# A decoder layer in fp32: how the down projection's weight sums are stored and split, and from which queue gate/up's results are stored

## The chip, the cores and the metric

The kernel runs on one core of a Trainium2 chip. The metric is the device time of one execution in microseconds (us). A core has five engines that work side by side, each through its own list of instructions in order: TensorE (PE) multiplies, VectorE (DVE) and ScalarE (ACT) do element-wise work, GpSimd (POOL) does some of it too, and SyncE (SP) mostly issues transfers. Transfers can be issued from SP, ACT and POOL. An engine that meets an instruction whose inputs are not ready waits there, with everything behind it.

## The reference

One layer of a hybrid decoder runs over 512 prompt tokens and 8 decode tokens, all in float32, with a model width of 2048 and an FFN width of 5632:

```
h = h + [gated delta net(x) ; multi-scale pooling(x)] @ w_out      with x = rmsnorm(h)
h = h + (silu(x2 @ w_gate) * (x2 @ w_up)) @ w_down                 with x2 = rmsnorm(h)
y = rmsnorm(h)
```

The outputs are y for both sets of tokens and the new recurrent, convolution and pooling states. The change touches the second line alone: gate/up is a product of 520 tokens with 2048 x 11264 weights, down one with 5632 x 2048.

## The kernel before, in words

Every float32 operand is split in two parts, hi (a copy rounded to the PE's format, cast by ACT, L1263) and lo (what is left, a subtraction by DVE, L1264). A product is then three passes: hi by hi, hi by lo, lo by hi (`passes`, L1270 to L1272), each a matmul of a 128 x 128 weight block with 260 tokens. Both FFN products use Strassen's scheme in Winograd's form: a pair of output columns times two halves of the tokens is computed with seven products M1 to M7 instead of eight. The weight sides of these are A11, A12, A22 and the sums S1 to S4 (made by DVE in `add`, L1299); the activation sides are B11, B21, B22 and T1 to T4, called forms (`FORM`). `strassen` (L1409) runs the products; at product i it cuts (splits into hi and lo) the weight of product i + 3 and makes the sum for i + 4, and at products 0, 2, 3 and 4 of a pair SP issues the loads A21, A11, A22 and A12 of the next pair. A pair is seven products, of 24 matmuls each in gate/up.

Gate/up has 22 blocks of FFN columns, each with a gate pair and an up pair (`gu`). After the up pair DVE multiplies the two (`gated`, L1460), POOL makes the four T forms of the result by subtraction (`to_dram`, L1466 to L1468) and stores all eight forms in DRAM (`a_d`, L1469, 1040 KB), issued from POOL. `hidden` is the hook that places this and other side work between products.

The down projection is cut along its inner dimension into three parts of 7, 7 and 8 blocks (`SIZES`), each with eight pairs. The forms of a part are loaded from `a_d` by `fetch` (L1824) and split by `fill` (ACT L1833, DVE or POOL L1835). So that forms can be replaced, the last pair of a stage is computed as eight plain products (`plain`), and meanwhile `cross` fetches and splits the next forms. There are three such crossings: from gate/up to part 0, and between the parts. The first pair of a part uses sums made ahead: during gate/up `sums_ahead` loads its blocks, makes S1 to S4 and stores seven blocks in DRAM (`near_d`); at the crossing SP reads them back (L1288), and they are split there and during that first pair, which goes in the order M4, M7, M1, M6, M5, M2, M3. In the first crossing the last `gated` and `to_dram` run too, and behind them POOL issues the loads of the residual h_d (`residual`, L2120: 12 of 260 KB, eight into mixb, four into mixa, which still holds what L1469 stores).

Names in the profile: raw, hi and lo are weight blocks (three buffers each, plus a fourth set from `xcp`); sg also holds A21; mixa and mixb are large buffers used for several things; dn and mm are PE's output banks; b11, b21, B22 and T1 to T4 with h or l are the forms.

Of the kernel before, what the change touches and what calls it, by code (L numbers as in the profile page):

```python
# [8 lines left out]
F32 = mybir.dt.float32  # L9
# [60 lines left out]
def decoder_kernel(ctx, tc, x_prompt, x_sample, state_delta, state_conv, state_pool, norm_mix, w_in,  # L70
# [1173 lines left out]
    BLOCKS = ("A11", "A12", "A22", "S1", "S2", "S3", "S4")  # L1244
# [4 lines left out]
    near_d = dram.tile([len(SIZES), 7, P, HG * P], F32, name="near_d")  # L1249
# [24 lines left out]
    class Pair:  # L1274
# [6 lines left out]
        def load(self, name, t=None):  # L1281
            if self.near is None:
                self.raw[name] = load_raw(self.view(int(name[1]) - 1, int(name[2]) - 1), t)
                return
            if t is None:
                t = wpl.tile([P, HG * P], F32, tag="raw", name="raw")
            self.raw[name] = t[:, :self.width]
            sp.dma_start(self.raw[name], self.near[BLOCKS.index(name), :, :self.width])  # L1288

        def cut(self, name, pool_=wpl):  # L1290
            self.w[name] = cut_raw(self.raw[name], pool_)

# [116 lines left out]
    def strassen(pairs, r21, hook, extra, order=FIRST):  # L1409

        steps = [(q, n) for q in range(len(pairs)) for n in (
            CROSSED if pairs[q].near is not None else order if q == len(pairs) - 1 else STEADY)]

        def block(i):
            return (pairs[steps[i][0]], FORM[steps[i][1]][0]) if i < len(steps) else (None, "")

        for i, (q, n) in enumerate(steps):  # L1420
            j = i % 7
            hook(q, j)
            if q + 1 < len(pairs):
                swap = q + 2 == len(pairs) and order is FIRST
                name = {0: "A21", 2: "A11", 3: "A12" if swap else "A22", 4: "A22" if swap else "A12"}.get(j)
                if name:
                    pairs[q + 1].load(name, r21 if name == "A21" else None)
            (p, name), (p4, name4) = block(i + 3), block(i + 4)
            pool_ = extra if i % 4 == 0 else wpl
            if p4 and p4.near is not None:  # L1430
                name4 = ""
            lastly = isinstance(p4 or p, LastPair)
            if name4 in ("S1", "S2", "S3") and not lastly:
                p4.add(name4)
            if name and (name != "S4" or lastly):
                p.cut(name, pool_)
            if name4 == "S4" or name4[:1] == "S" and lastly:
                p4.add(name4)
            pairs[q].multiply(n)
            pairs[q].combine(n)  # L1440
            if name == "S4" and not lastly:
                p.cut(name, pool_)
# [20 lines left out]
    def to_dram(fp):  # L1463
# [5 lines left out]
        pool.dma_start(a_d[:, :, fp, :].rearrange("q p c -> p q c"), q)  # L1469
# [336 lines left out]
    gu[2].add("S3")  # L1806
    up_out(0, 0, cm[:, 0, :], h1[0])
    gu[2].cut("A22")
    gu[2].load("A12")
    up_out(0, 1, cm[:, 0, :], c1[0])  # L1810
    gu[2].cut("S3")
# [15 lines left out]
    def fill(name, part_, rs=range(0, HG, 2), high=True, eng=dve):  # L1827
        hi, lo = forms[name]
        for r in rs:
            x = slice(r, min(r + 2, SIZES[part_]))  # L1830
            raw = lo[:, x, :].bitcast(F32)
            if high:
                act.copy(hi[:, x, :], raw)  # L1833
            if eng:
                eng.tensor_tensor(lo[:, x, :], raw, hi[:, x, :].bitcast(F32), op=ALU.subtract)  # L1835
# [68 lines left out]
    def run(pairs, r21, hook=None, order=FIRST, last=None, part_=None):  # L1904

        def during(q, j):
            if hook:
                hook(q, j)
            if pairs[0].near is not None and q == 0:
                if j == 2:  # L1910
                    fill("B21", part_)
# [10 lines left out]
    def ahead_of_cross(j, part_, last, r21):  # L1922
# [7 lines left out]
        elif j < 5:  # L1930
            fetch({2: "T4", 3: "T3", 4: "T2"}[j], part_) if j > 1 else None
        elif j == 5:
            first.load("A22")
            last.cut("A11")
            fill("T4", part_)
# [6 lines left out]
    def cross(part_, last):  # L1942
# [3 lines left out]
        def hook(step):  # L1946
# [3 lines left out]
            elif step == 1:  # L1950
                fill("B11", part_, eng=None)
            elif step == 2:
                first.cut("A22")
                fetch("T1", part_)
                fill("B11", part_, (0, 2), False, pool)
            elif step == 3:
                first.cut("S3")
                fetch("B21", part_)
                fill("B11", part_, (4,), False, pool)
            else:  # L1960
                first.cut("A11")
                fetch("B22", part_)
                fill("B11", part_, (6,), False, pool)
# [13 lines left out]
    def sums_ahead(part_):  # L1977
# [6 lines left out]

        def store(name, i):
            sp.dma_start(p.near[BLOCKS.index(name), :, :n], r[i])

        for i, name in enumerate(("A11", "A21", "A22", "A12")):
            sp.dma_start(r[i].rearrange("p (k c) -> p k c", c=P), p.view(int(name[1]) - 1, int(name[2]) - 1))
            yield  # L1990
        yield
        for i, name in ((0, "A11"), (2, "A22"), (3, "A12")):
            store(name, i)
            yield
        for name, *args in (("S3", 1, 0, 1, ALU.subtract), ("S2", 2, 2, 1, ALU.subtract), ("S1", 0, 2, 0, ALU.add),
                            ("S4", 3, 3, 2, ALU.subtract)):
            join(*args)
            yield
            store(name, args[0])

    def hidden(q, j):
# [5 lines left out]
        if j == (1 if q % 2 else 4):  # L2007
# [117 lines left out]
    to_dram(FP - 1)  # L2125
    for part_ in range(1, len(SIZES)):
# [71 lines left out]
```

## Time and profile before

| what | value |
|---|---|
| time, median of 3 runs | 2148.35 us (2147.03 to 2149.63) |
| the profiled execution | 2150.31 us, of which the span (first to last instruction) is 2148.5 us |
| mean granted PE clock | 0.998 |
| PE busy | 2120.6 us, 17680 matmuls |
| DVE, ACT, POOL busy | 1784.7, 934.3, 481.8 us |

W_out, the input projection and the mixing end at about 820 us; gate/up runs from there to about 1655, the first crossing to 1681, then come the parts of the down projection and the crossings between them. In a timeline row the first number is the start, the second the duration, and the bracket at the end holds the time that the engine stood idle before it and what ended that. Where several instructions of one kind follow each other, a row takes them together (x2, x3) and its second number is the time from the first one's start to the last one's end. SPq and POOLq rows are issues of transfers, not the transfers.

### The profile page before, as it was taken

What the parts mean: (1) busy time and instruction counts of PE and PEld (TensorE: products, weight loads), DVE (VectorE), ACT (ScalarE), POOL (GpSimd) and SP (SyncE); (2) the same over time, 40 slices, a digit from 0 to 9 for tenths busy, and PEclk for the clock granted to TensorE, in tenths of its full rate; (3) what the DMA queues carried; (4) which work ended last, traced back from release to release, by engine and by line L of the source; (5) the groups of instructions that cost most, each with busy time, mean ns of one, the idle gap of its engine ahead of it and who ended that gap; (6) DMA issues with size and microseconds to landing.
All of it is one profiled execution on the core that took longest, in us unless ns stands there. A gap on an engine that the chain in (4) does not pass through costs nothing.

```text
span 2148.5 us, 42900 instructions
## 1 busy us (share of the span) xinstructions
PE 2120.6 (99%) x17680; PEld 2106.6 (98%) x17680; DVE 1784.7 (83%) x2647; ACT 934.3 (43%) x1410; POOL 481.8 (22%) x572
## 2 busy tenths in 40 slices
PE   8999999999999999999999999999999999999998
PEld 7999999999999999999999999999999999999998
DVE  7786767666599979989988889888877898988997
ACT  6523443432255444434433434434434445435544
POOL 3212320222012202333233243232121302002100
PEclk9999999999999999999999999999999999999999
DMA  8344434434445535565575556565557737347333
GB/s 283 92 114 113 120 104 113 117 110 109 129 132 161 154 103 142 161 188 158 157 196 166 160 175 186 166 178 149 155 152 230 226 104 241 113 112 273 89 109 119
DMA packets 453569, 325.62 MB, mean 152 GB/s; under 512 B 27836, under 2 KB 424533, under 8 KB 452845
## 3 DMA queue, kind: packets, MB, share of 16 engines
q1 hardware_dynamic: 428781, 240.13, 39.2%
q0 software_dynamic: 23280, 81.94, 12.3%
q8 instruction: 139, 2.28, 0.4%
q10 hardware_dynamic: 1312, 0.80, 0.1%
q14 instruction: 57, 0.47, 0.1%
HBM read 265.76 MB, written 57.72 MB: 151 GB/s over the span
## 4 chain that ended last, share of the span: by engine, by line
PE 80%; DVE 11%; DMA 3%; issue 2%; ACT 2%; POOL 1%; SPq 0%; DVEq 0%; ACTq 0%; POOLq 0%
PE dn L1272 19%; PE dn L1270 19%; PE dn L1271 19%; PE mm L168 6%; PE mm L170 5%; PE mm L169 5%; DVE lo L1264 3%; DVE raw L1299 1%; DMA raw<-in_w_gate_up_dram 1%; DVE lo L137 1%; PE dn L870 1%; ACT hi L1263 1%; DMA qk<-tok_d 1%; DVE xl L195 0%; DMA xt<-in_x_prompt_dram 0%
## 5 line engine op out<-in xcount | busy, mean ns | idle before, releaser
L1264 DVE TENSOR_TENSOR lo<-raw,hi 128x1024 fp32r<-128x1024 f32 (+1 forms) x434 | 558.0, 1306 | 90.2 <-ACT hi L1263 88.7
L1263 ACT CAST hi<-raw 128x1024 fp32r<-128x1024 f32 (+1 forms) x434 | 438.4, 1025 | 427.6 <-DVE raw L1299 239.6
L168 PE MATMUL mm<-xh,hi 128*128 128x256 f32 (+1 forms) x1280 | 377.6, 295 | 2.8 <-DVE mixa L259 2.8
L170 PE MATMUL mm<-xh,lo 128*128 128x256 f32 (+1 forms) x1280 | 362.9, 284 | 0.4 <-DVE lo L137 0.4
L169 PE MATMUL mm<-xl,hi 128*128 128x256 f32 (+1 forms) x1280 | 362.6, 283 | 0.4
L168 PEld LDWEIGHTS mm<-xh,hi 128*128 128x128 f32 x1280 | 242.6, 190 | 6.6 <-DVE mixa L259 3.3
L169 PEld LDWEIGHTS mm<-xl,hi 128*128 128x128 f32 x1280 | 242.8, 190 | 1.0 <-DVE xl L350 1.0
L170 PEld LDWEIGHTS mm<-xh,lo 128*128 128x128 f32 x1280 | 242.0, 189 | 0.6 <-DVE lo L137 0.6
L1299 DVE TENSOR_TENSOR raw<-raw 128x1024 f32<-128x1024 f32 (+1 forms) x130 | 177.2, 1363 | 2.2
L1271 PE MATMUL dn<-b21l,hi 128*128 128x260 f32 x598 | 169.4, 283 | 0.0
L1272 PE MATMUL dn<-b21h,lo 128*128 128x260 f32 x598 | 169.3, 283 | 0.0
L1272 PE MATMUL dn<-b11h,lo 128*128 128x260 f32 x590 | 167.1, 283 | 1.7 <-DVE lo L1264 1.7
L1270 PE MATMUL dn<-b21h,hi 128*128 128x260 f32 x598 | 168.7, 282 | 0.0
L1271 PE MATMUL dn<-b11l,hi 128*128 128x260 f32 x590 | 167.1, 283 | 0.0
L1270 PE MATMUL dn<-b11h,hi 128*128 128x260 f32 x590 | 166.6, 282 | 0.0
L1466 POOL TENSOR_TENSOR mixa<-mixa 128x520 f32<-128x520 f32 x22 | 55.6, 2528 | 461.7 <-DVE mixa L1460 461.7
L1270 PE MATMUL dn<-T1h,hi 128*128 128x260 f32 x534 | 151.9, 284 | 0.0
L1271 PE MATMUL dn<-T1l,hi 128*128 128x260 f32 x534 | 151.5, 284 | 0.0
L1272 PE MATMUL dn<-B22h,lo 128*128 128x260 f32 x526 | 148.6, 283 | 2.6 <-DVE lo L1264 2.6
L1272 PE MATMUL dn<-T1h,lo 128*128 128x260 f32 x534 | 150.6, 282 | 0.0
L135 ACT CAST hi<-raw 128x1024 fp32r<-128x1024 f32 (+2 forms) x86 | 87.2, 1015 | 144.4 <-PE mm L169 141.8
L1270 PE MATMUL dn<-B22h,hi 128*128 128x260 f32 x526 | 149.6, 284 | 0.0
(653 smaller groups left out, 6570.3 us busy)
## 6 DMA issues: line engine op xcount, KB each, us to landing
raw<-in_w_gate_up_dram SPq DMA_DIRECT2D x134, 512.0 KB
raw<-in_w_in_dram SPq DMA_DIRECT2D x79, 512.0 KB
a_d<-mixa POOLq DMA_DIRECT2D x22, 1040.0 KB, 7.7
mixb<-in_w_gate_up_dram SPq DMA_DIRECT2D x41, 512.0 KB
raw<-in_w_down_dram SPq DMA_DIRECT2D x42, 448.0 KB
raw<-in_w_out_dram SPq DMA_DIRECT2D x25, 512.0 KB
raw<-in_w_down_dram SPq DMA_DIRECT2D x21, 512.0 KB
raw<-near_d SPq DMA_DIRECT2D x14, 448.0 KB
```

What stands on the lines that cost most here:

```text
L135: act.copy(hi[:, r], raw[:, r])
L137: dve.tensor_tensor(lo[:, r], raw[:, r], hi[:, r].bitcast(F32), op=ALU.subtract)
L168: te.matmul(acc[ci], wh, hi[k][:, c0:c1], start=(k == 0), stop=False)
L169: te.matmul(acc[ci], wh, lo[k][:, c0:c1], start=False, stop=False)
L170: te.matmul(acc[ci], wl, hi[k][:, c0:c1], start=False, stop=(k == len(w) - 1))
L1263: act.copy(hi, raw)
L1264: dve.tensor_tensor(lo, raw, hi.bitcast(F32), op=ALU.subtract)
L1270: te.matmul(acc, wh[:, k, :], xf[:, k, :], start=start and k == 0, stop=False)
L1271: te.matmul(acc, wh[:, k, :], xg[:, k, :], start=False, stop=False)
L1272: te.matmul(acc, wl[:, k, :], xf[:, k, :], start=False, stop=stop and k == wh.shape[1] - 1)
L1299: dve.tensor_tensor(r[name], r[a], r[b], op=op)
L1466: pool.tensor_tensor(q[:, 4:8:2, :], q[:, 1:4:2, :], q[:, 0:2, :], op=ALU.subtract)
```

## The change

Five things are done. The stored sums: `near_d` holds S1 to S4 only, A11, A12 and A22 of a part's first pair are read from the weights themselves, and `sums_ahead` is spread over other places of gate/up, with its loads and stores behind A12's load. A stored sum is split in place (`cut_sum`): hi goes into a new tile, lo over the raw block. S3 and S2 are split in the crossing, S1, A12 and S4 at the first three products of the first pair. `fill` splits a form in two pieces (blocks 0 to 3, and the rest) instead of four, and all subtractions are DVE's, B11's too, which POOL did before. The store of `a_d` moves from POOL to SP (`keep`): behind the last load (A12) of the next gate pair, and for the last block directly behind `to_dram` in the program. And at the start of gate/up, A22's cut and A12's load come ahead of the addition and the cut of S3.

```diff
-    near_d = dram.tile([len(SIZES), 7, P, HG * P], F32, name="near_d")
+    near_d = dram.tile([len(SIZES), 4, P, HG * P], F32, name="near_d")
...
+        def cut_sum(self, name, pool_=wpl, tag="hi"):
+
+            raw = self.raw[name]
+            hi = pool_.tile([P, HG * P], F32R, tag=tag, name=tag)[:, :raw.shape[1]]
+            act.copy(hi, raw)
+            lo = raw.bitcast(F32R)
+            dve.tensor_tensor(lo, raw, hi.bitcast(F32), op=ALU.subtract)
+            self.w[name] = [x.rearrange("p (k c) -> p k c", c=P) for x in (hi, lo)]
...
+        phase = 0 if pairs[0].near is None else 3
...
-            pool_ = extra if i % 4 == 0 else wpl
+            pool_ = extra if i % 4 == phase else wpl
             if p4 and p4.near is not None:
                 name4 = ""
+            if p and p.near is not None:
+                name = ""
...
-        pool.dma_start(a_d[:, :, fp, :].rearrange("q p c -> p q c"), q)
+
+    def keep(fp):
+        sp.dma_start(a_d[:, :, fp, :].rearrange("q p c -> p q c"), quarters)
...
-    gu[2].add("S3")
-    up_out(0, 0, cm[:, 0, :], h1[0])
     gu[2].cut("A22")
     gu[2].load("A12")
+    gu[2].add("S3")
+    gu[2].cut("S3")
+    up_out(0, 0, cm[:, 0, :], h1[0])
     up_out(0, 1, cm[:, 0, :], c1[0])
-    gu[2].cut("S3")
     gu[2].add("S2")
...
-    def fill(name, part_, rs=range(0, HG, 2), high=True, eng=dve):
+    def fill(name, part_):
         hi, lo = forms[name]
-        for r in rs:
-            x = slice(r, min(r + 2, SIZES[part_]))
+        for x in (slice(0, 4), slice(4, SIZES[part_])):
             raw = lo[:, x, :].bitcast(F32)
-            if high:
-                act.copy(hi[:, x, :], raw)
-            if eng:
-                eng.tensor_tensor(lo[:, x, :], raw, hi[:, x, :].bitcast(F32), op=ALU.subtract)
+            act.copy(hi[:, x, :], raw)
+            dve.tensor_tensor(lo[:, x, :], raw, hi[:, x, :].bitcast(F32), op=ALU.subtract)
...
+                if j == 0:
+                    pairs[0].cut_sum("S1", xcp)
+                if j == 1:
+                    pairs[0].cut("A12")
                 if j == 2:
+                    pairs[0].cut_sum("S4", xcp, "lo")
                     fill("B21", part_)
...
-            elif step == 1:
-                fill("B11", part_, eng=None)
             elif step == 2:
+                fetch("T1", part_)
                 first.cut("A22")
-                fetch("T1", part_)
-                fill("B11", part_, (0, 2), False, pool)
+                fill("B11", part_)
             elif step == 3:
-                first.cut("S3")
                 fetch("B21", part_)
-                fill("B11", part_, (4,), False, pool)
-            else:
+                first.cut_sum("S3")
+                first.cut_sum("S2", tag="lo")
+            elif step == 4:
+                fetch("B22", part_)
                 first.cut("A11")
-                fetch("B22", part_)
-                fill("B11", part_, (6,), False, pool)
                 fill("T1", part_)
...
+        load("A11", 0)
+        load("A21", 1)
+        yield
+        yield
+        yield
+        load("A22", 2)
+        load("A12", 3)
+        yield
+        join(1, 0, 1, ALU.subtract)
+        yield
+        join(2, 2, 1, ALU.subtract)
+        yield
+        store("S3", 1)
+        store("S2", 2)
+        yield
+        join(0, 2, 0, ALU.add)
+        yield
+        join(3, 3, 2, ALU.subtract)
+        yield
+        store("S1", 0)
+        store("S4", 3)
...
+        if j == 5 and q % 2 == 0:
+            keep(q // 2)
+        if j in (1, 2, 5) and q % 2:
...
     to_dram(FP - 1)
+    keep(FP - 1)
```

How the rows move, at three places. First DVE at the start of gate/up, where L1299 (L1305 after) is an addition for a sum, L1264 (L1263) a subtraction for lo and L1450 (L1459) an addition of the up half; before:

```order
L1653 TENSOR_TENSOR T4l<-mixb,T4h 128x520 x2
L1299 TENSOR_TENSOR mixa<-raw,mixa 128x1024
L1450 TENSOR_TENSOR mixa<-cm,dn 128x260
L1264 TENSOR_TENSOR lo<-raw,hi 128x1024
L1450 TENSOR_TENSOR mixa<-cm,mm 128x260
L1264 TENSOR_TENSOR lo<-mixa,hi 128x1024
L1299 TENSOR_TENSOR raw<-raw,mixa 128x1024
L1450 TENSOR_TENSOR mixa<-cm,dn 128x260 x2
L1299 TENSOR_TENSOR raw<-raw 128x1024
L1264 TENSOR_TENSOR lo<-raw,hi 128x1024
L1460 TENSOR_TENSOR mixa<-mixa,sg 128x1040
```

and after:

```order
L1664 TENSOR_TENSOR T4l<-mixb,T4h 128x520 x2
L1263 TENSOR_TENSOR lo<-raw,hi 128x1024
L1305 TENSOR_TENSOR mixa<-raw,mixa 128x1024
L1263 TENSOR_TENSOR lo<-mixa,hi 128x1024
L1459 TENSOR_TENSOR mixa<-cm,dn 128x260
L1459 TENSOR_TENSOR mixa<-cm,mm 128x260
L1305 TENSOR_TENSOR raw<-raw,mixa 128x1024
L1459 TENSOR_TENSOR mixa<-cm,dn 128x260 x2
L1305 TENSOR_TENSOR raw<-raw 128x1024
L1263 TENSOR_TENSOR lo<-raw,hi 128x1024
L1469 TENSOR_TENSOR mixa<-mixa,sg 128x1040
```

The subtraction for A22 has moved to the front, and S3's follows the addition of S3 directly. Next SP over some pairs of gate/up with side work; before:

```order
L1255 DMA raw<-in_w_gate_up_dram 128x8x128 x3
L1255 DMA mixb<-in_w_gate_up_dram 128x8x128
L1255 DMA raw<-in_w_gate_up_dram 128x8x128 x2
L1986 DMA near_d<-mixb 128x896
L1255 DMA raw<-in_w_gate_up_dram 128x8x128
L1255 DMA mixb<-in_w_gate_up_dram 128x8x128
L1986 DMA near_d<-mixb 128x896
L1255 DMA raw<-in_w_gate_up_dram 128x8x128 x3
L1255 DMA mixb<-in_w_gate_up_dram 128x8x128
L1255 DMA raw<-in_w_gate_up_dram 128x8x128 x2
```

and after:

```order
L1254 DMA mixb<-in_w_gate_up_dram 128x8x128
L1254 DMA raw<-in_w_gate_up_dram 128x8x128 x3
L1480 DMA a_d<-mixa 128x8x260
L1254 DMA mixb<-in_w_gate_up_dram 128x8x128
L1254 DMA raw<-in_w_gate_up_dram 128x8x128 x3
L1998 DMA mixb<-in_w_down_dram 128x7x128
L1998 DMA mixa<-in_w_down_dram 128x7x128
L1254 DMA mixb<-in_w_gate_up_dram 128x8x128
```

The store a_d (before on POOL) stands here between the last of a pair's loads (raw x3 are A11, A22 and A12) and the first load of the next pair (mixb is A21); the side loads L1998 stand there in other pairs. The third place is SP in the first crossing, from the last loads of gate/up; before:

```order
L1255 DMA mixb<-in_w_gate_up_dram 128x8x128
L1255 DMA raw<-in_w_gate_up_dram 128x8x128 x2
L1288 DMA raw<-near_d 128x896 x7
L1255 DMA sg<-in_w_down_dram 128x7x128
L1255 DMA raw<-in_w_down_dram 128x7x128 x3
L1255 DMA sg<-in_w_down_dram 128x7x128
```

and after:

```order
L1254 DMA raw<-in_w_down_dram 128x7x128
L1285 DMA raw<-near_d 128x896
L1254 DMA raw<-in_w_down_dram 128x7x128
L1285 DMA raw<-near_d 128x896 x2
L1254 DMA raw<-in_w_down_dram 128x7x128
L1285 DMA raw<-near_d 128x896
L1480 DMA a_d<-mixa 128x8x260
L1254 DMA sg<-in_w_down_dram 128x7x128
L1254 DMA raw<-in_w_down_dram 128x7x128 x3
L1254 DMA sg<-in_w_down_dram 128x7x128
```

The store of the last a_d stands ahead of the loads of the second down pair (sg is its A21, the raw behind it A11, A22 and A12). The loads of the first pair come in turns from near_d and from the weights.

More of the change, by code (lines that the diff above doesn't have):

```diff
@@ L1243, in decoder_kernel @@
     LASTLY = ("M1", "M7", "M6", "M5", "M3", "M2", "M4")
-    BLOCKS = ("A11", "A12", "A22", "S1", "S2", "S3", "S4")
     CROSSED = ("M4", "M7", "M1", "M6", "M5", "M2", "M3")
@@ L1281, in load @@
         def load(self, name, t=None):
-            if self.near is None:
+            if name[0] == "A":
                 self.raw[name] = load_raw(self.view(int(name[1]) - 1, int(name[2]) - 1), t)
                 return
-            if t is None:
-                t = wpl.tile([P, HG * P], F32, tag="raw", name="raw")
             self.raw[name] = t[:, :self.width]
-            sp.dma_start(self.raw[name], self.near[BLOCKS.index(name), :, :self.width])
+            sp.dma_start(self.raw[name], self.near[int(name[1]) - 1, :, :self.width])
         def cut(self, name, pool_=wpl):
             self.w[name] = cut_raw(self.raw[name], pool_)
+        def cut_sum(self, name, pool_=wpl, tag="hi"):
[5 more added lines that the diff above has]
+            self.w[name] = [x.rearrange("p (k c) -> p k c", c=P) for x in (hi, lo)]
         def add(self, name):
@@ L1930, in ahead_of_cross @@
         elif j < 5:
-            fetch({2: "T4", 3: "T3", 4: "T2"}[j], part_) if j > 1 else None
+            if j > 1:
+                fetch({2: "T4", 3: "T3", 4: "T2"}[j], part_)
+            if j == 4:
+                fill("T4", part_)
         elif j == 5:
@@ L1934, in ahead_of_cross @@
             last.cut("A11")
-            fill("T4", part_)
         else:
@@ L1983, in join, with load @@
             dve.tensor_tensor(r[i], r[a], r[b], op=op)
+        def load(name, i):
+            sp.dma_start(r[i].rearrange("p (k c) -> p k c", c=P), p.view(int(name[1]) - 1, int(name[2]) - 1))
         def store(name, i):
[L1986 to L1990, printed above, removed]
+            sp.dma_start(p.near[int(name[1]) - 1, :, :n], r[i])
         yield
[L1992 to L1999, printed above, removed]
+        yield
[17 more added lines that the diff above has]
+        join(3, 3, 2, ALU.subtract)
+        yield
+        store("S1", 0)
+        store("S4", 3)
+        yield
     def hidden(q, j):
@@ L2006, in hidden @@
             next(states[q // 2])
-        if j == (1 if q % 2 else 4):
+        if j == 5 and q % 2 == 0:
+            keep(q // 2)
+        if j in (1, 2, 5) and q % 2:
             next(ahead, None)
```

## The prediction

> **What bounds the kernel now.** I read the page's engine shares and its chain of waits first, then the stretches of 100 us, then what PE waits for, and last the timeline round each wait.
>
> ```profile
> span 2148.5 us, 42900 instructions
> PE 2120.6 (99%) x17680; PEld 2106.6 (98%) x17680; DVE 1784.7 (83%) x2647; ACT 934.3 (43%) x1410; POOL 481.8 (22%) x572
> ...
> L1264 DVE TENSOR_TENSOR lo<-raw,hi 128x1024 fp32r<-128x1024 f32 (+1 forms) x434 | 558.0, 1306 | 90.2 <-ACT hi L1263 88.7
> ```
>
> ```profile
> core 0: us, PE busy (x) PEld busy (x) DVE busy (x) ACT busy (x) POOL busy (x), PEclk, DMA share, GB/s
> 1600.00:1700.00 100.00, 98.34 (x814) 97.86 (x813) 79.90 (x99) 47.07 (x71) 35.84 (x45) 1.00 0.73 232
> 1700.00:1800.00 100.00, 100.00 (x833) 100.00 (x833) 89.37 (x128) 39.20 (x47) 3.77 (x7) 1.00 0.49 140
> ```
>
> ```profile
> engine line waited for: us in total, times, longest us
> PE dn L1272 <- DVE lo L1264: 6.6, 10, 1.2
> ```
>
> PE is busy in 99% of the span. At full speed 100 us hold 833 matmuls, 0.120 us each; none is added or removed by the change, so the time moves only by the stalls of PE. The waits view, taken from 560 us to the end, gives ten of them for a split weight block (the low half, lo), 6.6 us together. These are the stalls that matter here:
>
> ```profile
> 826.07 0.39 PE L1272 MATMUL dn<-T4h,lo 128*128 128x260 f32 x1 [1.03 <-DVE lo L1264]
> ...
> 1174.28 0.39 PE L1272 MATMUL dn<-T3h,lo 128*128 128x260 f32 x1 [0.23 <-DVE lo L1264]
> ...
> 1458.63 0.39 PE L1272 MATMUL dn<-T3h,lo 128*128 128x260 f32 x1 [0.79 <-DVE lo L1264]
> ...
> 1695.86 0.39 PE L1272 MATMUL dn<-B22h,lo 128*128 128x260 f32 x1 [1.25 <-DVE lo L1264]
> ...
> 1987.33 0.39 PE L1272 MATMUL dn<-B22h,lo 128*128 128x260 f32 x1 [0.94 <-DVE lo L1264]
> ...
> 1999.35 0.39 PE L1272 MATMUL dn<-T2h,lo 128*128 128x260 f32 x1 [0.22 <-DVE lo L1264]
> ```
>
> Each costs about 0.27 us more than the idle time in its bracket: the waiting matmul starts late behind its drained predecessor (0.28 us long, 0.12 us apart) and is 0.1 us slow itself. 1.25 is thus a loss of 1.52. Even if every stall left after 820 us went, no more than some 8 us could be won: 6.6 less the 1.12 of one wait at 637 us, plus nine times 0.27. A loss has no such bound.
>
> **The gate/up start (A22 ahead of S3).**
>
> ```profile
> 823.33 1.22 DVE L1299 TENSOR_TENSOR mixa<-raw,mixa 128x1024 f32<-128x1024 f32 x1
> 824.46 0.42 DVE L1450 TENSOR_TENSOR mixa<-cm,dn 128x260 f32<-128x260 f32 x1
> 824.80 1.22 DVE L1264 TENSOR_TENSOR lo<-raw,hi 128x1024 fp32r<-128x1024 f32 x1
> ...
> 830.35 1.21 DVE L1264 TENSOR_TENSOR lo<-raw,hi 128x1024 fp32r<-128x1024 f32 x1
> ...
> 824.71 1.04 ACT L1263 CAST hi<-mixa 128x1024 fp32r<-128x1024 f32 x1 [1.07 <-DVE mixa L1299]
> ```
>
> Now S3's add (L1299, 823.33) and one addition of the up half (L1450) stand ahead of A22's split (824.80), for which PE waits at 826.07. Moved first, A22's split starts when its cast is done, about 823.65, and PE's 1.29 is gone. What is late next: S3's add then runs 824.80 to 826.02, ACT casts it in 1.05 to 827.1, and only then can DVE split it, to 828.35. DVE executes in order, and the next row is that split, so it stands idle for 1.1 us. The L1450 that empties the bank into which the third product (M7) writes ends at 828.7 instead of 824.9; M7 is due at 828.81 − 1.29 = 827.5, so it waits 1.1. Behind it stand S2's add, two L1450, S1's add and S2's split: 0.34 + 1.13 + 0.67 + 1.14 + 1.21 brings S2 to 833.1, where M6, one product of 2.88 us after M7's late start, wants it at 831.6. Together 2.6 against 1.29 before, and a later B22 0.2 worse: **+1.5** (from −1.3, should the bank be free sooner, to +2.2).
>
> **Gate/up: the store behind the loads.**
>
> ```profile
> 1157.26 0.92 POOL L1469 DMA_DIRECT2D a_d<-mixa  x1 [0.59 <-POOL mixa L1468]
> ...
> 1157.78 5.67 SPq L1255 DMA_DIRECT2D raw<-in_w_gate_up_dram  x2
> 1178.46 5.21 SPq L1255 DMA_DIRECT2D raw<-in_w_gate_up_dram  x3
> ...
> 1167.96 1.05 ACT L1263 CAST hi<-raw 128x1024 fp32r<-128x1024 f32 x1 [2.99 <-DMA raw<-in_w_gate_up_dram]
> ...
> 1186.29 1.06 ACT L1263 CAST hi<-raw 128x1024 fp32r<-128x1024 f32 x1 [2.77 <-DMA raw<-in_w_gate_up_dram]
> ```
>
> The 1040 KB store starts with the load of A22: that load is cast 10.2 us after its issue (1157.78 to 1167.96), a lone one 2.6 us after (the last of three issues ends at 1178.46 + 5.21 = 1183.67). The stalls at 1171 to 1177 (three, 0.9 together) and at 1458 (0.79 + 0.36 with its follower) come of it. On SP behind the last load of a pair, the store is over before the next pair's block is wanted: **−1.9**, bounds 0 (the store meets another transfer) and −2.1. The fewer and rarer transfers of the sums hide behind PE; without that cover each is a load like the one above.
>
> **First crossing to the down projection, DVE's side.**
>
> ```profile
> 1670.91 2.57 POOL L1835 TENSOR_TENSOR b11l<-b11l,b11h 128x520 fp32r<-128x520 f32 x2
> ...
> 1671.47 2.96 DVE L1264 TENSOR_TENSOR lo<-raw,hi 128x896 fp32r<-128x896 f32 x1 [0.66 <-ACT hi L1263]
> ...
> 1676.70 2.29 DVE L1264 TENSOR_TENSOR lo<-raw,hi 128x896 fp32r<-128x896 f32 x1
> ...
> 1682.26 1.24 DVE L1460 TENSOR_TENSOR mixa<-mixa,sg 128x1040 f32<-128x1040 f32 x1
> ...
> 1694.72 2.08 DVE L1264 TENSOR_TENSOR lo<-raw,hi 128x896 fp32r<-128x896 f32 x2
> ```
>
> Beside POOL's pieces of B11 a split of 896 takes 2.96 and 2.29 instead of 1.04 (half of 2.08): 3.2 lost, and 0.7 on a form. In two pieces on DVE, B11 costs 1.16 + 0.87 = 2.0 by the widths of L1460. DVE is some 1.9 ahead, the last gate product (1682.26) starts near 1680.3, and S4, split in the 2.08 that B22 waits for at 1695.86, is split a product earlier: **−1.5** there and **−0.2** at small stalls about 1659. In place or not, a split has the same width, so I cost that at 0. On the other side S4 and A12 now precede B21's pieces, two splits of 1.04 against the lead of 1.9: were B21 only just in time before, 0.2 + 0.27 is lost there.
>
> **First crossing, SP's side.** This is the largest term.
>
> ```profile
> 1684.01 7.30 SPq L1255 DMA_DIRECT2D raw<-in_w_down_dram  x3
> ...
> 1687.32 1.09 POOL L1468 TENSOR_TENSOR mixa<-mixa 128x260 f32<-128x260 f32 x1
> 1688.70 0.93 POOL L1469 DMA_DIRECT2D a_d<-mixa  x1 [0.30 <-POOL mixa L1468]
> 1689.63 3.72 POOL L2120 DMA_DIRECT2D mixb<-h_d  x7
> ...
> 1690.13 0.95 ACT L1263 CAST hi<-raw 128x896 fp32r<-128x896 f32 x1 [0.19 <-DMA raw<-in_w_down_dram]
> ```
>
> ```profile
> q0 software_dynamic: 664, 2.23, 83.5%
> q1 hardware_dynamic: 627, 0.31, 16.3%
> ```
>
> Before, the second down pair's A21 and A11 are issued from 1683.5 on, and A11 is cast at 1690.13. After, the last store of the gated activations stands on SP ahead of them, and SP waits in it until POOL is through with its subtractions. That is 4.9 us after the gate product (1682.26 + 1.24 to 1688.41), with DVE ahead at X = 1686.3 (bounds 1685.5 and 1688.4). At X POOL also issues its twelve loads of h_d, 260 KB each. What the two queues get then, the DMA view of 1697 to 1704 shows, where A21 of the third pair meets the last of those loads: 664 software packets of 3.36 KB (83.5% of 16 engines x 7 us, 141 ns each) against 627 of 512 B from SP (29 ns), one for one.
>
> The sum: data flows some 1.2 us after an issue starts (the lone load above: 2.6 from the issue's end to the cast, less 64 packets per engine at 29 ns, 1.9, plus the issue, 0.5 by 3.72 / 7). The store is 64 rows of 1040 B per engine; a row takes between 29 ns (like 512 B) and 58 (in proportion), say 45. Eight h_d loads are 40 software packets per engine, alternating with 40 store rows: 40 x 0.186 = 7.4, then 24 x 0.045 = 1.1; the store ends at X + 9.7. A21 and A11 follow with 56 packets each at 29 ns, 3.2; the last four h_d loads, freed by the store's end, put in up to 20 x 0.141 = 2.8, of which I take half: X + 14.3 = 1700.6. Cast of 0.95: PE's M1 of the second pair can start at 1701.6. It is due at 1696.7 (B22's last product without its stall), so 4.9 idle; A11's lo (1.04) comes one more split later, and A22, 1.6 behind A11, costs 0.5 at M4: **+6.5**. Bounds: without h_d's packets A11 lands at X + 1.2 + 2.9 + 3.2 + 0.9 = 1694.5 and nothing waits (0); with X = 1688.4 and all of the 2.8, +10.
>
> ```profile
> 124.78:128.19 3.41, 1.62 (x14) 1.46 (x13) 3.27 (x10) 1.38 (x3) 0.00 (x0) 1.00 0.51 140
> 128.19:131.60 3.41, 3.41 (x19) 3.41 (x18) 3.27 (x7) 0.41 (x1) 0.00 (x0) 0.50 0.14 29
> 131.60:135.01 3.41, 3.41 (x30) 3.41 (x30) 3.14 (x9) 1.06 (x1) 0.00 (x0) 1.00 0.47 138
> ```
>
> A gap of 4.9 us also touches the clock. Early in this kernel a stretch of 3.41 us in which PE was busy for 1.62 is followed by one at a granted clock of 0.50, with 19 matmuls where a full one has 28.4: 9.4 x 0.12 = **+1.1** (0 if the gap is short).
>
> [...]
>
> The first pair's own A11, A12 and A22 now come in rows of 512 B: 56 x 29 ns = 1.6 us each, hidden behind the product or more (2.5 us) between their issue and their cast; without that cover a late one costs PE up to the 1.6.
>
> **Second and third crossing.** No store stands there. Between 1700 and 1800 us PE misses nothing. The third crossing's stalls at 1987 and 1999 (1.21 and 0.48) are of the kind cured above, 1.69 together, of which I take **−1.4**, since B21's pieces stand later there too (bounds −1.7 and +0.5).
>
> **The sum** against the profiled run: 1.5 − 1.9 − 0.2 − 1.5 + 6.5 + 1.1 − 1.4 = **+4.1 us**. That run took 2150.31 with a span of 2148.5; the median of the runs shown is 2148.35, so the differences are put on the median: **2152.4**.
>
> **The rivals.**
>
> *The loads land in time.* If the store's rows and SP's loads pass the software packets faster than one for one, A11 is there by 1695.7; the crossing then costs 0, the clock nothing, and 4.1 − 7.6 = −3.5 is left: 2144.9, or 2143.5 if the start is not worse. For it speaks that SP's queue alone moves 1 MB in under 4 us at 29 ns per 512 B; against it the one-for-one row, and 44 KB per us for SP in it.
>
> [...]
>
> *A short stall.* X at 1685.5 and h_d's loads late or half as dense: some 3 us of waiting, no halved clock: −3.5 + 3.5 = 0, 2148.4.
>
> *Gate/up's gain does not come.* POOL's loads of the sample states and the state's store, which shared those engines before, or the moved store itself, meet a weight load: −1.9 becomes 0 to +1, 2154.5. Nothing in the trace places such a load at that point, so it is the least likely.
>
> **How the numbers follow.** The forecast 0.45 (2150.5 to 2155), loads in time 0.2, a short stall 0.2, no gain in gate/up 0.15. Two tenths of a per cent, 4.3 us, is about what a measurement of this kernel tells from no change. Faster than 2144.05: part of the second, 0.1. Slower than 2152.65: half of the forecast, most of the last and a tail of 10-us stalls, 0.45. Within: 0.45. The range is 2144.5 to 2157: its low end leaves out the lower half of the loads in time, its high end the forecast with the stall's bound of 10 and half of gate/up lost.
>
> **What would show it.** In the profile after: SP's issue of the store at about 1686 ahead of the loads of the second pair, PE waiting there for ACT's cast of A11 until about 1701, followed by a stretch at half clock; two waits at 828 and 832 in place of the one at 826; no waits at 1171 to 1177, 1458, 1695 and 1987. A cast of A11 before 1697 would make the forecast wrong at its main term; so would fewer than 820 matmuls per 100 us anywhere between 860 and 1640.

## The result, and the profile after

The changed kernel takes 2172.28 us (median of 4 runs, 2168.58 to 2174.0) against 2148.99 for the kernel before in the same comparison: a ratio of 1.0107, 95% interval 1.009 to 1.0125. That is 23.3 us slower. The forecast was 2152.4 within 2144.5 to 2157: slower by some 4 us, where it is more than five times as much.

The head of the page of the changed kernel:

```profile
span 2170.9 us, 42811 instructions
PE 2126.5 (98%) x17680; PEld 2111.2 (97%) x17680; DVE 1777.0 (82%) x2617; ACT 929.9 (43%) x1368; POOL 445.8 (21%) x538
```

The same 17680 matmuls stand in a span that is 22.4 us longer, and every engine but PE is busy for less time than before. So no work was added: PE waits, or runs at a lower clock. PE's waits from 560 us on, and stretches of 100 us in the same columns as before:

```profile
PE dn L1269 <- ACT hi L1262: 11.6, 4, 10.1
PE dn L1271 <- DVE lo L1263: 8.6, 9, 2.1
PE dn L1269 <- DVE mixa L1459: 1.1, 1, 1.1
```

```profile
1100.00:1200.00 100.00, 100.00 (x833) 100.00 (x832) 90.90 (x97) 40.06 (x48) 31.38 (x23) 1.00 0.60 177
...
1600.00:1700.00 100.00, 98.09 (x798) 97.47 (x796) 72.99 (x82) 43.19 (x54) 28.06 (x37) 0.98 0.69 216
1700.00:1800.00 100.00, 89.69 (x721) 89.39 (x722) 80.60 (x115) 36.17 (x42) 1.10 (x3) 0.93 0.44 124
1800.00:1900.00 100.00, 97.57 (x797) 97.13 (x797) 84.15 (x118) 45.60 (x55) 7.51 (x14) 0.98 0.56 174
1900.00:2000.00 100.00, 97.76 (x798) 97.33 (x797) 83.97 (x113) 46.53 (x53) 7.42 (x14) 0.98 0.65 202
```

A new kind of wait is on top: for ACT's cast, 10.1 us at once. From 900 us to the end of gate/up every 100 us now hold 832 or 833 matmuls. What loses, besides the start of gate/up, is the stretches with a crossing (the first crossing lies in two of them), and their granted clock (the third number from the end) is below 1.00.

A table helps to compare. For each stretch it holds the sum of what the starts of PE's matmuls lie further apart than 0.12 us, worked out from the trace (a wait counts, and the slow restart behind it, where the next start comes 0.22 us later, as at 832.48 and 832.70, and a halved clock, with starts 0.22 us apart):

| stretch, us | what it holds | before | changed | difference |
|---|---|---|---|---|
| 820 to 860 | start of gate/up | 2.1 | 4.9 | +2.9 |
| 860 to 1650 | gate/up | 5.4 | 3.2 | −2.1 |
| 1650 to 1680 | first crossing, its start | 1.0 | 4.0 | +3.1 |
| 1680 to 1730 | first and second down pair | 1.7 | 13.7 | +12.0 |
| 1815 to 1860 | second crossing (before: from 1800) | 0.2 | 4.5 | +4.3 |
| 1960 to 1995 | third crossing | 1.3 | 4.4 | +3.1 |

These make 23.3; all the rest of the kernel differs by −0.9 together.

The start of gate/up in the changed kernel, PE's two waits there and DVE's rows:

```profile
828.16 0.36 PE L1269 MATMUL dn<-T3h,hi 128*128 128x260 f32 x1 [1.13 <-DVE mixa L1459]
...
832.48 0.39 PE L1271 MATMUL dn<-T2h,lo 128*128 128x260 f32 x1 [0.94 <-DVE lo L1263]
...
823.99 1.22 DVE L1305 TENSOR_TENSOR mixa<-raw,mixa 128x1024 f32<-128x1024 f32 x1
826.45 1.23 DVE L1263 TENSOR_TENSOR lo<-mixa,hi 128x1024 fp32r<-128x1024 f32 x1 [1.25 <-ACT hi L1262]
827.60 0.42 DVE L1459 TENSOR_TENSOR mixa<-cm,dn 128x260 f32<-128x260 f32 x1
```

DVE stands idle for 1.25 us behind S3's addition, the third product waits 1.13 for its bank and S2 is late by 0.94.

The first crossing, at the second down pair: SP's and POOL's issues, ACT's cast of A11, and PE:

```profile
1689.77 0.37 SPq L1480 DMA_DIRECT2D a_d<-mixa  x1
1690.19 0.57 SPq L1254 DMA_DIRECT2D sg<-in_w_down_dram  x1
1690.87 14.09 SPq L1254 DMA_DIRECT2D raw<-in_w_down_dram  x3
...
1688.26 1.48 POOL L1477 TENSOR_TENSOR mixa<-mixa 128x260 f32<-128x260 f32 x1
1689.68 4.27 POOL L2149 DMA_DIRECT2D mixb<-h_d  x8
...
1709.00 0.94 ACT L1262 CAST hi<-raw 128x896 fp32r<-128x896 f32 x1 [17.08 <-DMA raw<-in_w_down_dram]
...
1709.99 0.58 PE L1269 MATMUL dn<-b11h,hi 128*128 128x260 f32 x1 [10.06 <-ACT hi L1262]
```

SP issues nothing until POOL's subtraction ends, as forecast; A11 is cast 19.2 us after the store's issue.

And the second crossing, ACT and PE in the changed kernel:

```profile
1810.52 0.94 ACT L1262 CAST hi<-raw 128x896 fp32r<-128x896 f32 x1 [2.52 <-DVE raw L1305]
1817.08 1.93 ACT L1842 CAST T4h<-T4l 128x1040 fp32r<-128x1040 f32 x2 [5.62 <-DMA T4l<-a_d]
1818.92 0.94 ACT L1262 CAST hi<-raw 128x896 fp32r<-128x896 f32 x1
...
1819.91 0.39 PE L1269 MATMUL dn<-b11h,hi 128*128 128x260 f32 x1 [0.29 <-ACT hi L1262]
1822.56 0.59 PE L1271 MATMUL dn<-b11h,lo 128*128 128x260 f32 x1 [2.14 <-DVE lo L1263]
```

against ACT in the kernel before:

```profile
1796.94 0.94 ACT L1263 CAST hi<-raw 128x896 fp32r<-128x896 f32 x1 [0.46 <-PE dn L1271]
1800.99 1.16 ACT L1833 CAST T4h<-T4l 128x520 fp32r<-128x520 f32 x2 [3.11 <-DMA T4l<-a_d]
```

Before, ACT cast A11 of the plain pair first and waited for the form T4 afterwards, when nothing that was due at once stood behind it. Now ACT waits 5.62 us for T4's transfer, and A11 (1818.92) is behind that; DVE's part of A11 comes later still (1821.42), behind T4's subtractions (1818.18). This is a wait that the prediction has no word for. It comes from a few lines of the change that moved T4's split one product forward. They are neither among the five points of the section on the change nor in the lines shown there; the first experiment shows them.

### The profile page after: what moved, and what is told of

The parts are those of the page before. It is cut to its first block, busy times and chain, and to the rows that moved or that the text cites. A ratio compares the mean times of both kernels' runs of the same rounds, so it can differ in the third digit from the quotient of the medians.

```text
span 2170.9 us, 42811 instructions
## 1 busy us (share of the span) xinstructions
PE 2126.5 (98%) x17680; PEld 2111.2 (97%) x17680; DVE 1777.0 (82%) x2617; ACT 929.9 (43%) x1368; POOL 445.8 (21%) x538
## 4 chain that ended last, share of the span: by engine, by line
PE 80%; DVE 8%; issue 7%; DMA 3%; ACT 1%; POOL 1%; SPq 0%; DVEq 0%; ACTq 0%; POOLq 0%
PE dn L1269 19%; PE dn L1270 19%; PE dn L1271 19%; PE mm L168 5%; PE mm L170 5%; PE mm L169 5%; DVE lo L1263 2%; DMA T4l<-a_d 1%; DVE lo L137 1%; PE dn L870 1%; PE mm L1269 1%; PE mm L1270 1%; PE mm L1271 1%; DVE raw L1305 1%; DMA qk<-tok_d 0%
## 5 line engine op out<-in xcount | busy, mean ns | idle before, releaser
L1263 DVE TENSOR_TENSOR lo<-raw,hi 128x1024 fp32r<-128x1024 f32 (+1 forms) x422 | 545.2, 1312 | 87.7 <-ACT hi L1262 86.2
L1262 ACT CAST hi<-raw 128x1024 fp32r<-128x1024 f32 (+1 forms) x422 | 426.8, 1027 | 421.8 <-DVE raw L1305 228.2
L1269 PE MATMUL dn<-b11h,hi 128*128 128x260 f32 x590 | 170.0, 288 | 11.5 <-ACT hi L1262 11.4
L1305 DVE TENSOR_TENSOR raw<-raw 128x1024 f32<-128x1024 f32 (+1 forms) x130 | 167.2, 1286 | 2.2
L1456 ACT ACTIVATE sg<-sg 128x260 f32<-128x260 f32 x88 | 37.0, 422 | 266.4 <-DVE sg L1455 266.4
L1271 PE MATMUL dn<-T1h,lo 128*128 128x260 f32 x512 | 144.4, 282 | 0.0
L137 DVE TENSOR_TENSOR lo<-raw,hi 128x1024 fp32r<-128x1024 f32 (+2 forms) x87 | 102.1, 1175 | 51.6 <-ACT hi L135 50.1
```

The costliest lines, as they stand in the source:

```text
L137: dve.tensor_tensor(lo[:, r], raw[:, r], hi[:, r].bitcast(F32), op=ALU.subtract)
L1262: act.copy(hi, raw)
L1263: dve.tensor_tensor(lo, raw, hi.bitcast(F32), op=ALU.subtract)
L1269: te.matmul(acc, wh[:, k, :], xf[:, k, :], start=start and k == 0, stop=False)
L1271: te.matmul(acc, wl[:, k, :], xf[:, k, :], start=False, stop=stop and k == wh.shape[1] - 1)
L1305: dve.tensor_tensor(r[name], r[a], r[b], op=op)
```

## The experiments

Each is timed against the kernel before on the same chip; that kernel took 2148.85, 2150.15 or 2150.77 us there, so times of different groups are compared by their distance to it. The changed kernel is 23.3 us above.

**T4 behind A11 again.** In the changed kernel, at the end of the pairs before a crossing:

```diff
             if j > 1:
                 fetch({2: "T4", 3: "T3", 4: "T2"}[j], part_)
-            if j == 4:
-                fill("T4", part_)
         elif j == 5:
             first.load("A22")
             last.cut("A11")
+            fill("T4", part_)
```

> The changed kernel with one thing put back: at each crossing the split of T4 stands behind the split of the last pair's A11 again, not one product ahead of it. Theory T4: the cast of T4 waits for its transfer from DRAM (ACT stood 5.62 us for it at 1817) and holds A11's cast behind it in ACT's list. The losses at 1650 to 1680, 1815 to 1860 and 1960 to 1995 (4.05, 4.46 and 4.41 us against 0.98, 0.16 and 1.34 before) should go, about -10 us: 2162 (2160 to 2164), with PE's waits at 1656, 1822 and 1970 gone. Rival: DVE is late because all of B11 and two more sums are its work now; then the place of T4 changes little, -1 us or less.

Measured: 2160.22 us (2159.44 to 2161.01), 11.4 above the kernel before, so 11.9 of the 23.3 are gone. The losses at the crossings' starts fall from 4.0, 4.5 and 4.4 to 0.8, 0.1 and 0.5. DVE still does all of B11 and the earlier sums in this kernel, so these are not what made it late.

**T4 ahead, in the kernel before.** The mirror of it, one part of the change alone:

```diff
             fetch({2: "T4", 3: "T3", 4: "T2"}[j], part_) if j > 1 else None
+            if j == 4:
+                fill("T4", part_)
         elif j == 5:
             first.load("A22")
             last.cut("A11")
-            fill("T4", part_)
```

> The kernel before with one part of the change alone: T4's split one product earlier, ahead of the split of the last pair's A11 (in four pieces, as before). Theory T4: this edit is enough by itself; it costs a wait of some 2 us and up to one stretch of 3.41 us at half clock (1.6 us) at each of three crossings: 2149 + 6 to + 10.5, so 2155 to 2160. Rival: it needs the rest of the change (B11 on DVE, two pieces) to hurt: 2151 or less.

Measured: 2160.83 us (2158.28 to 2164.6) against 2150.77: ratio 1.0048, interval 1.0035 to 1.0062. ACT and PE in this kernel:

```profile
1804.71 1.16 ACT L1833 CAST T4h<-T4l 128x520 fp32r<-128x520 f32 x2 [3.98 <-DMA T4l<-a_d]
...
1807.21 0.94 ACT L1263 CAST hi<-raw 128x896 fp32r<-128x896 f32 x1
...
1955.55 0.39 PE L1270 MATMUL dn<-b11h,hi 128*128 128x260 f32 x1 [1.17 <-ACT hi L1263]
1957.74 0.39 PE L1272 MATMUL dn<-b11h,lo 128*128 128x260 f32 x1 [1.68 <-DVE lo L1264]
```

So the edit is enough by itself to cost 10 us. In the profiled execution the starts of the three crossings lose 7.3 of it, without a halved stretch; 1.2 more are lost in gate/up and 1.4 behind 1995, which the profile does not tie to the edit.

**The last store on POOL.** In the changed kernel, POOL issues the last store as in the kernel before:

```diff
     to_dram(FP - 1)
-    keep(FP - 1)
+    pool.dma_start(a_d[:, :, FP - 1, :].rearrange("q p c -> p q c"), quarters)
```

> The changed kernel with one thing put back: the last store of the activations is issued from POOL, ahead of h_d's loads, and SP's loads for the second down pair no longer stand behind it. Theory SP: the wait of SP's list behind the store is what makes A11 late (cast at 1709.0). The loss of 13.7 us between 1680 and 1730 should fall to under 1.5, -12 to -13 us: 2159.5 (2158 to 2162). Rival: h_d's twelve loads, issued beside the weights' loads, are the cause wherever the store stands; then A11 stays late by 5 us or more and the time is above 2164.

Measured: 2157.94 us (2154.17 to 2160.4), 9.1 above the kernel before, 14.2 less than the changed kernel. The loss between 1680 and 1730 is 0.2.

**The last store on SP, behind the loads.**

```diff
     to_dram(FP - 1)
-    keep(FP - 1)
...
     def residual(q, j):
+        if (q, j) == (0, 5):
+            keep(FP - 1)
```

> The changed kernel with the last store still on SP, but behind the second down pair's four loads instead of ahead of them. Theory: the place in SP's list is what costs, since SP waits in the store until POOL is through; with the loads ahead of it the loss of 13.7 us at 1680 to 1730 goes to under 1.5: -12 to -14, 2159 (2157 to 2161), like the store on POOL. Rival: a store on the hardware queue beside h_d's loads delays later loads wherever it stands: a stall of 3 us or more at A12 or at the third pair, above 2162.

Measured: 2156.28 us (2155.84 to 2158.89) against 2150.15, so 6.1 above and 17.2 less than the changed kernel, about as with the store on POOL (of the 3 us between the two, 1.4 stand at the starts of the crossings, where two stretches ran at half clock there and one here); the loss between 1680 and 1730 is 0.2 again. SP's issues:

```profile
1684.07 0.38 SPq L1254 DMA_DIRECT2D sg<-in_w_down_dram  x1
1684.56 4.09 SPq L1254 DMA_DIRECT2D raw<-in_w_down_dram  x3
1689.36 1.33 SPq L1480 DMA_DIRECT2D a_d<-mixa  x1
```

The loads go out 5 us before the store could. A store on SP's queue does no harm here; its place in SP's list did.

**h_d without a software queue.** In the changed kernel the store stays ahead of the loads, and h_d's loads go to SP:

```diff
-                pool.dma_start(mix[m], h_d[m])
+                (sp if q >= 0 else pool).dma_start(mix[m], h_d[m])
```

> The changed kernel, the store still on SP ahead of the loads, but h_d's twelve loads are issued from SP, two with each pair and behind that pair's A21, so that no software queue shares the engines with the weights' loads. Theory SP alone (the list's wait until POOL is through sets A11's time): A11 stays as late as the wait, cast near 1702 or later, less than 4 us gained. Theory of both (the wait leaves 10 us, which the store and the loads alone would fit into, and the software packets take it away): A11 lands some 9 to 10 us after the store's issue, at about 1699.5, and PE waits 1 us or less there: -11 us, 2161 (2159 to 2163.5).

Measured: 2159.9 us (2158.37 to 2161.4), 11.1 above the kernel before, 12.2 gained. PE's wait is in between the two theories, well below 10 us and well above the 1 us expected:

```profile
1702.26 0.58 PE L1269 MATMUL dn<-b11h,hi 128*128 128x260 f32 x1 [2.97 <-ACT hi L1262]
```

A11 was cast at 1701.26, 12.2 us after the store's issue at 1689.10, with two of h_d's loads ahead of it in the list. So of the 10 us wait, 7 need the software queue beside SP's, and 3 come without it, from the wait in SP's list and the two loads. These shares do not add up in any order: with SP's loads ahead of the store, the software queue cost nothing (0.2 in the two runs above). How the two queues shared, by the DMA view of the changed kernel, first from 1690 to 1695, then from 1698 to 1703 us, then, with h_d's loads nearly done, from 1707 to 1709:

```profile
q1 hardware_dynamic: 957, 1.00, 72.1%
q0 software_dynamic: 79, 0.27, 13.5%
```

```profile
q0 software_dynamic: 480, 1.59, 81.6%
q1 hardware_dynamic: 573, 0.29, 20.3%
...
q1 hardware_dynamic: 1153, 0.58, 111.1%
q0 software_dynamic: 11, 0.01, 1.9%
```

While the store runs, only 79 of h_d's packets pass, though POOL issued from 1689.68 on. From 1698 to 1703 it is 96 software packets per us, when A21 and A11 are under way, against 115 of SP's: its queue gets 0.06 MB per us, and 0.29 as soon as it is alone.

**The start of gate/up as before.** The six lines at the start of gate/up put back in the changed kernel.

```diff
-    gu[2].cut("A22")
-    gu[2].load("A12")
     gu[2].add("S3")
-    gu[2].cut("S3")
     up_out(0, 0, cm[:, 0, :], h1[0])
+    gu[2].cut("A22")
+    gu[2].load("A12")
     up_out(0, 1, cm[:, 0, :], c1[0])
+    gu[2].cut("S3")
```

> The changed kernel with only the start of gate/up put back (S3's addition and a part of the up half ahead of A22's split). The trace of the changed kernel loses 4.93 us between 820 and 860 against 2.07 before, by two waits at 828 and 832 and two at 841 and 843. Theory: the order causes it, through DVE's idle time behind S3's addition: 2172.3 - 2.2 = 2170.1 (the run with all three put back lost 2.75 there). Rival: the place costs nothing by itself, the later pairs would absorb it: 2172.

Measured: 2169.14 us (2167.25 to 2172.14), 19.0 above the kernel before, 4.3 less than the changed kernel. The trace gives the start 2.3 of it (4.9 to 2.7). At the starts of the three crossings, which the edit does not touch, the profiled execution loses 9.3 instead of 12.9, with two of the three halved stretches gone; so by the profiled execution the rest of the 4.3 is the clock, and not the start.

**Three put back.** T4 behind A11, the last store on POOL, the old start:

> The changed kernel with three things put back: T4's split behind A11's, the last store on POOL, and S3 ahead of A22 at the start of gate/up. If the three losses are separate they add up: 2172.3 - 10 - 12.5 - 2.9 = 2146.9 (2144 to 2149), 2 us faster than the kernel before, from gate/up (-2.1) and from S4's earlier split at the first and third crossing (-1.5 and -1.2). Rival: what is left of the change loses elsewhere once these stalls are gone (B21's pieces behind S4 and A12 come late): 2149 to 2152.

Measured: 2145.16 us (2143.86 to 2146.84) against 2148.85: ratio 0.9983, interval 0.9974 to 0.9992. Taken singly the three gave 11.9, 14.2 and 4.3 us, 30.4 together; at once they give 27.0. Later, on another chip and beside the last variant below ("the variant above" in the text that follows):

> The version with three things put back once more, beside the two variants of it on one chip, since those ran on another. If B11 on POOL or on DVE makes no difference, as the stalls of the traces say (2.7 and 2.6 us after 815), this is within 0.7 us of the variant above; if the 2 us between their ratios to the kernel before are real, it is 2 us slower.

2145.53 us (2143.99 to 2145.79) against 2150.77: ratio 0.9974, interval 0.9964 to 0.9984. It is within 0.2 us of that variant. So what is left of the change gains 3.7 to 5.2 us. All of PE's waits after 860 us, in the first of the two:

```profile
PE dn L1271 <- DVE lo L1263: 0.3, 1, 0.3
```

**Gate/up's stores on POOL again,** in that version (the store goes back to the end of `to_dram`, and `keep` is not called):

```diff
         pool.tensor_tensor(q[:, 7, :], q[:, 2, :], q[:, 5, :], op=ALU.subtract)
+        pool.dma_start(a_d[:, :, fp, :].rearrange("q p c -> p q c"), q)
...
-        if j == 5 and q % 2 == 0:
-            keep(q // 2)
```

> The version with three things put back, and gate/up's stores issued from POOL right behind the subtractions again, as in the kernel before; the sums keep their new places. Theory: the store's place cured gate/up's stalls (2.1 us, at 1171 to 1177 and 1458), so the loss between 860 and 1650 goes back from 3.25 to about 5.3: 2147.2. Rival: the rarer and later transfers of the sums cured them; then it stays at 2145.2.

Measured: 2147.74 us (2146.34 to 2148.72) against 2150.15, so 2.4 below it, where the version with the stores on SP is 3.7 to 5.2 below, and its variant with B11 on POOL, on the same chip as this one, 5.7. The loss between 860 and 1650 is 6.1 instead of 3.3, with waits like those of the kernel before, in other pairs:

```profile
1252.39 0.39 PE L1271 MATMUL dn<-T4h,lo 128*128 128x260 f32 x1 [0.99 <-DVE lo L1263]
1255.76 0.39 PE L1271 MATMUL dn<-T3h,lo 128*128 128x260 f32 x1 [0.22 <-DVE lo L1263]
```

The store's place gives gate/up's gain; the sums' new places do not.

**B11 on POOL,** in the version with three put back:

```diff
-    def fill(name, part_):
+    def fill(name, part_, eng=dve):
...
-                fill("B11", part_)
+                fill("B11", part_, pool)
```

> The version with three things put back, with B11's lo made by POOL again, in two pieces. It tells apart what cured the waits of PE for B22 at 1695 and 1987 (1.52 and 1.21 us). Theory S4: the earlier split of S4 did, so no wait of PE comes back at S4's product and the time is 2145.2 to 2146. Rival POOL: the splits of DVE that took 2.96 and 2.29 us beside POOL's pieces were what made DVE late; then 1 to 3 us come back: 2146.5 to 2148.

Measured: 2144.43 us (2143.55 to 2145.33) against 2150.15. No wait returns: behind 860 us PE has the same single one of 0.3. DVE's splits of S3 and of S4 in the crossing, and the first matmul that takes the low half of S4 (it lies over the raw block):

```profile
1668.05 4.67 DVE L1296 TENSOR_TENSOR raw<-raw,hi 128x896 fp32r<-128x896 f32 x1 [1.81 <-ACT hi L1294]
...
1682.07 1.63 DVE L1296 TENSOR_TENSOR raw<-raw,lo 128x896 fp32r<-128x896 f32 x1
...
1691.04 0.28 PE L1271 MATMUL dn<-B22h,raw 128*128 128x260 f32 x1
```

Beside POOL, which splits B11 from 1667.49 on for 4.27 us, a split of DVE still takes 4.67 us, and PE does not wait for it. So B11 on DVE is worth nothing. S4 is split 7.3 us before PE needs it, where in the kernel before it was split while PE waited (the row at 1694.72). That is what cured the wait at 1695, and by the same order the one at 1987; S4's place was not put back by itself.

**A22 between S3's addition and the up half,** with B11 on POOL:

```diff
     gu[2].add("S3")
-    up_out(0, 0, cm[:, 0, :], h1[0])
     gu[2].cut("A22")
     gu[2].load("A12")
+    up_out(0, 0, cm[:, 0, :], h1[0])
     up_out(0, 1, cm[:, 0, :], c1[0])
     gu[2].cut("S3")
```

> The three things put back and B11's lo on POOL, and at the start of gate/up A22's split directly behind S3's addition, ahead of both additions of the up half (instead of between them). Theory: DVE is never idle there and A22's split comes 0.34 us sooner, so PE's wait for it falls from 1.04 to about 0.7 and nothing else moves: 0.3 us faster than the same without it, which only the trace can tell; about 2144.1. Rival: the bank that the up half empties is late by as much and the third product waits.

Measured: 2145.36 us (2143.71 to 2146.51) against 2150.77, ratio 0.9975 (0.9965 to 0.9985). The start loses 2.1 instead of 2.7: the first wait falls from 1.04 to 0.71 as expected. Other waits moved too: the one for B22 rose from 0.41 to 0.61, and one of 0.22 for T3 went. This and the other two versions beat both kernels, and cannot be told apart by their times.

## Why the prediction was wrong

Two steps failed. T4's move, which cost some 10 to 12 us, is in no term of the sum. And SP's side of the first crossing, with its clock, was mis-sized: 13.5 us for 7.6. The start of gate/up, 2.9 for 1.5, is a third and smaller miss. The terms one by one:

**What bounds the kernel** was right: time moves by PE's stalls alone, a gain is bounded by 8 us and a loss is not.

**The start, +1.5:** the right mechanism (DVE idle 1.25 for the forecast 1.1, the bank's wait 1.13 for 1.1, S2's wait 0.94 for 1.5), but mis-sized: 2.9, of which 2.3 are the order by itself. The two waits together came out as forecast, 1.3 us worse. The term for what follows, "a later B22 0.2 worse", measured 0.8 (waits of 0.18 and 0.75 against 0.40, and a slow restart behind each). A further wait of 0.21 for T3, which loses 0.6 with its restarts, stays when the order is put back. It is gone with gate/up's stores on POOL, and also with A22 between, so it takes the moved stores and one of these orders together.

**Gate/up, −1.9:** right, −2.1, and by the cause named.

**First crossing, DVE's side, −1.5 − 0.2:** the wait at 1695 went, as forecast, but not for the reason that took most of the working. POOL beside DVE was not the cost: B11 back on POOL brought no wait back, and S4 split earlier is enough. And the small stalls about 1659 became 1.08 and 0.76 by T4.

**First crossing, SP's side, +6.5:** the right mechanism, mis-sized: with the clock's share 13.5 (13.7 lost between 1680 and 1730, against 0.2 with the store on POOL) for 7.6, and a wait of 10.06 for 4.9. The wait for POOL is in place (the store's issue was put 10.4 us ahead of the time at which A11 is due, and stood 10 ahead). What failed is the step "Eight h_d loads are 40 software packets per engine, alternating with 40 store rows". The 79 packets counted while the store ran are 5 per engine. The other 55 came from 1695 on, when A21, A11 and A22 were on their way, where the sum has "up to 20" and takes half. (The store itself was through sooner than in the sum, 1695 to 1696, 6 us behind X and not 9.7.) A11 came at X + 19.2 instead of X + 14.3. The same row that gave one for one gave the right price, once the software queue was running; that it started late was not in any row quoted. The experiments show a way out: with the store behind the loads, or on POOL, nothing of this is lost.

**The clock, +1.1:** mis-sized twice. The 19 matmuls of the halved stretch are those that overlap it, and by that count a stretch at full clock has 30 (the row behind it), not 28.4. By starts, 0.217 us apart instead of 0.120, it is 16 for 28: 1.5 us. And after the long wait four stretches of 3.41 us were halved, the last two with PE at work again (last section): between 1709.99 and 1716.28 only 26 matmuls started where 52 fit at full clock, 3.2 us.

**Second and third crossing, 0 and −1.4:** wrong in sign, +4.3 and +3.1. "No store stands there" was true and beside the point. The −1.4 itself was right: with the three put back, the stalls at 1987 and 1999 are gone and that stretch loses 1.7 less than before. The step that failed is one that is not there: of the moved pieces of `fill`, T4's was not followed to the engine's list. What the prediction itself took for SP (an engine that waits holds everything behind it, and SP did issue nothing until 1689.77) gives it at once for ACT: ACT waited 3.11 us for T4 in the kernel before, with A11's cast done 3 us earlier, so exchanging the two puts a cast that is due at once behind a wait that was harmless. T4 alone accounts for 10 to 12 of the 23 us (11.9 won by putting it back, 10.1 lost by moving it alone).

**The rivals:** none of them happened. The loads did not land in time, the stall was not short, and gate/up's gain came. Where both queues had much to move (SP's 20.3%, the software queue 81.6% of the 16 engines' time) their packets passed nearly one for one (573 to 480 between 1698 and 1703), as in the kernel before (627 to 664 between 1697 and 1704).

## What to carry to other kernels

When work is moved forward, follow each instruction of it to its engine's list and ask what it will wait for there and who stands behind it; an idle time that cost nothing (3.11 us of ACT before T4) becomes a stall for whatever is placed behind it. A store that has to wait for another engine belongs behind the loads in an issuing engine's list, or on the list of the engine that it waits for: that one place was worth 14 to 17 us here. A change of several parts that is slower as a whole can hold a gain: three small pieces put back turned +23 us into −4 to −5.

## What the runs showed of the hardware

**In these traces the clock was halved for whole stretches of 3.41 us on a fixed grid, behind stretches at full clock in which PE was busy for 1.70 us or less.** Rows of the changed kernel, three waits of about 2 us and the stretch behind each, cut on that grid (their starts lie 48 and 92 times 3.413 us behind the first):

```profile
1654.84:1658.25 3.41, 1.57 (x11) 1.17 (x11) 1.87 (x3) 1.77 (x4) 0.00 (x0) 1.00 0.74 261
1658.25:1661.66 3.41, 3.41 (x19) 3.41 (x18) 1.56 (x2) 1.78 (x4) 0.00 (x0) 0.50 0.80 233
...
1818.68:1822.09 3.41, 1.45 (x10) 1.02 (x8) 3.31 (x6) 3.41 (x5) 0.00 (x0) 1.00 0.49 166
1822.09:1825.50 3.41, 2.94 (x13) 2.94 (x14) 3.20 (x7) 1.99 (x3) 0.00 (x0) 0.50 0.52 167
...
1968.87:1972.28 3.41, 1.56 (x13) 1.56 (x14) 3.27 (x6) 3.41 (x4) 0.00 (x0) 1.00 0.36 107
1972.28:1975.69 3.41, 3.41 (x18) 3.41 (x17) 3.31 (x6) 1.86 (x4) 0.00 (x0) 0.50 0.88 269
```

The same wait at the third crossing with the old start (2.13 us, up to 1966.85) fell across two stretches:

```profile
1962.50:1965.95 3.45, 2.22 (x17) 1.83 (x15) 3.05 (x6) 3.45 (x5) 0.00 (x0) 1.00 0.86 314
1965.95:1969.36 3.41, 2.51 (x21) 2.51 (x21) 3.20 (x6) 2.65 (x3) 0.00 (x0) 1.00 0.55 173
1969.36:1972.77 3.41, 3.41 (x31) 3.41 (x30) 3.41 (x5) 2.68 (x4) 1.06 (x2) 1.00 0.93 256
```

Busy for 1.45 to 1.57 of 3.41 us: the next stretch was halved. Busy for 2.22 and 2.51: it was not. In all thirteen traces, from 60 us on and without the last stretches of the kernel, each stretch at full clock with PE busy for 1.63 or less was followed by a halved one, and none with 1.73 or more was; of one with 1.70 (the store behind the loads, 1653.74) and one with 1.71 (gate/up's stores on POOL, 125.49), the first was. So one and the same wait of 2.1 us cost 2.7 there and 4.4 in the changed kernel, by where on the grid it fell. Counted from the span's start, the edges of the grid lie at 1.9 us and whole stretches more in the trace of the kernel before (halved from 128.19 on), at 2.8 in that of the changed kernel (halved from 1658.25 on). It fits that the times of the changed kernel spread more (2168.58 to 2174.0) than those of the version with B11 on POOL (2143.55 to 2145.33). After the long wait two halved stretches ran on with PE at work:

```profile
1709.45:1712.86 3.41, 2.54 (x10) 2.25 (x11) 2.79 (x5) 1.43 (x2) 0.00 (x0) 0.50 0.11 27
1712.86:1716.28 3.42, 3.42 (x18) 3.42 (x18) 3.32 (x6) 1.04 (x2) 0.00 (x0) 0.50 0.00 0
```

18 matmuls overlap the second, where 31 overlap the stretch at full clock in the rows above. Behind a stretch that was itself halved the numbers were others: 2.54 busy was followed by one more at half clock here, 2.94 at 1822.09 was not.

**The software queue was slow to start here.** Eight loads were issued by POOL between 1689.68 and 1693.95, and by 1695 79 packets had passed. The store's traffic on the other queue was not enough to hold them back in another run: with the store behind the loads, 416 software packets passed beside 576 rows of the same store between 1694 and 1699, from 4.7 us after the first issue on. What held them back in the changed kernel, no run here settles.
